# Linear attention by chunk states, and its 32-row products two heads at a time, in a two-block network

## The chip, the cores and the metric

The kernel runs on one core of a Trainium2 chip. The metric is the device time of one launch in microseconds (us): 3082.91 us in the median of three runs (3081.30 to 3084.93). Times inside the launch come from one profiled execution, whose span from the first to the last instruction is 3080.9 us. PE is the matrix engine, DVE the vector engine, ACT the scalar engine, POOL GpSimd, SP the engine that issues most transfers.

## The reference, cut to what matters

The network has two blocks of two layers each over 512 tokens of width 1024. In each layer of the first block a mixing stage computes four branches side by side; the second of them is a gated linear attention with 4 heads (keys of 32, values of 64), run forward and backward over the tokens:

```python
def gla_scan(q, k, v, log_a, include_diag):
    def step(state, inp):
        qc, kc, vc, ac = inp
        b = jnp.cumsum(ac, axis=2)
        o_inter = jnp.einsum('bhtk,bhkv->bhtv', qc * jnp.exp(b), state)
        ...
        scores = jnp.einsum('bhtk,bhsk,bhtsk->bhts', qc, kc, decay)
        o = o_inter + jnp.einsum('bhts,bhsv->bhtv', scores, vc)
        b_last = b[:, :, -1:, :]
        state = jnp.exp(b_last[:, :, 0, :])[..., None] * state + \
            jnp.einsum('bhsk,bhsv->bhkv', kc * jnp.exp(b_last - b), vc)
        return state, o
...
    o_f = gla_scan(q, k, v, la_f, True)
    o_b = flip(gla_scan(flip(q), flip(k), flip(v), flip(la_b), False))
    o = (o_f + o_b).transpose(0, 2, 1, 3)
```

The other branches are a short convolution, a softmax attention of 4 heads and a convolution of width 31 with a layer norm. An output product, two layer norms and a feed-forward follow. The second block (attention over selected keys, a mixture of experts) is not touched.

## The kernel before

Everything in the mixing stage of a layer is traced by four generators that `merge` runs side by side, the one furthest behind its share next: `linear` (share 36), `mla` (the softmax attention, 29), `convolutions` (112, with the projections of the input) and `output` (18). The tile scheduler then sets each engine's order from that trace. A `Lane` holds the tiles of one generator: lane G of the linear attention has two banks of PSUM (`ps=2`), lanes A and M two each.

`gla_scores` makes A[s, head, t], the product of query t with key s under the decays between them, for all pairs of tokens by the largest power-of-two boundary between them. There are nine levels, m = 1, 2, ..., 256. For each, ACT takes exponentials (L937 to L942), DVE multiplies them onto q and k (L939, L943), and POOL and ACT bring the running sums to the next level (L957 to L970). In the seven levels below 128, `diag` makes 16 PE products per level (L906): per head, one bank with four blocks of 128 x 128 out of 32 rows (`tile_position=(32 * h, 0)`), then one DVE copy under a mask (COPY_PREDICATED, L913; at level 1 an ACT copy, L910, and L911). The levels 128 and 256 keep their scaled q and k as `far`.

`gla_out` handles one tile of 128 tokens: for each head three 32-row products against the other three tiles (L989), an ACT copy of them (L991), then one product of the tile's own scores with the values (L996) and three of the copied ones (L999), 64 columns each; then the norm and gate.

Operands here are in f32, and each f32 product of the program is two MATMUL records in the trace. The large products (L364 to L366, `mm3`) are three products of split halves, one record each. In a mixing stage these are the projections (`AP<-g,hi`), the output product (`AP<-hi,g`, 192 of them: `out_part` for two of the branches, then for the other two) and the values.

The width-31 convolution is 62 steps on DVE (L776, L778). Its layer norm starts on PE with L786 and on DVE with L789; the output product of its branch begins after that. `attended` and `output` close the stage.

Of the kernel before, what the change touches and what calls it, by code (L numbers as in the profile page):

```python
# [16 lines left out]
OP = mybir.AluOpType  # L17
# [31 lines left out]

def tok_units(w, c, kp):  # L50
    """Rows of two k tiles and 512 columns of w as a moving unit [128, 2 * 512]."""
# [8 lines left out]
def cols(v):  # L60
    """[n * 128] -> [128, n]"""
# [7 lines left out]
def layout(i):  # L69
# [66 lines left out]
    # second block  # L136
# [58 lines left out]
def shape_constants():  # L195
# [14 lines left out]
    # frequency, phase (of a cosine), sign  # L210
# [10 lines left out]
    c["rconst"] = r  # L221
    c["iota"] = np.broadcast_to(p.astype(np.float32), (128, 128))
# [26 lines left out]
def pipeline(n, *stages):  # L249
    """Stage s of item i beside stage s + 1 of item i - 1."""  # L250
# [8 lines left out]
class Lane:  # L259
    """Tiles of one chain of work: its own slots, so that chains do not wait for each other's."""  # L260
# [27 lines left out]
class Net:  # L288
# [20 lines left out]
    def part(self, name):  # L309
        """Room on chip for a part of the work."""  # L310
# [6 lines left out]
    def phase(self, name):  # L317
        """The same with banks of PSUM."""
# [3 lines left out]
    # ---- small helpers  # L322
# [9 lines left out]
    def room(self, dt):  # L332
        """Small tiles in one of the raw ones, until it is full."""
# [15 lines left out]
    def new_h(self):  # L349
        """Token-major tiles [4][128, 1024]."""  # L350
# [3 lines left out]
    def row(self, L, name, n):  # L354
        """A row of DRAM on every partition."""
# [5 lines left out]
    def mm3(self, ps, a, b, start, stop):  # L361
        """ps (+)= a.T @ b for operands (high, low)."""
# [5 lines left out]
    def split(self, hi, lo, src, engine=None):  # L368
        """hi + lo = src, in parts that the PE carries exactly."""
# [3 lines left out]
    def rsqrt(self, L, v, n, scale=1.0, add=EPS):  # L373
        """(v * scale + add) ** -0.5 of [128, n] (more than 0)."""
# [26 lines left out]
    # ---- layer norm of token-major tiles into token-major h and feature-major (high, low)  # L401
# [10 lines left out]
    def ln_norm(self, L, t, gb, spill=None, light=()):  # L412
        """The layer norm of h[t], in place."""
# [3 lines left out]
    def ln_stats(self, L, src):  # L417
        """Of rows in two halves: what normalises them."""
# [1586 lines left out]
```

## Time and profile before

| what | value |
|---|---|
| median of three runs | 3082.91 us (3081.30 to 3084.93) |
| profiled execution, first to last instruction | 3080.9 us |
| PE busy | 2959.6 us (96%) |
| DVE busy | 2155.6 us (70%) |
| ACT busy | 1432.6 us (46%) |
| POOL busy | 463.6 us (15%) |
| mixing stage of layer 0, first product of `diag` to the feed-forward | 63.52 to 330.21 us |
| the same of layer 1 | 742.75 to 1006.03 us |

The busy time of PE over the span says that it is seldom without work, not that every stage is limited by it. So each mixing stage is read in four stretches, cut where the work changes: from the first `diag` product to the input of the wide convolution (L731); from there to the layer norm behind it (L789); to the first output product; and to the feed-forward. For each the profile gives the busy time of every engine and the granted clock of PE.

### The profile page before, as it was taken

What the parts mean: (1) busy time and instruction counts of PE and PEld (TensorE: products, weight loads), DVE (VectorE), ACT (ScalarE), POOL (GpSimd) and SP (SyncE); (2) the same over time, 40 slices, a digit from 0 to 9 for tenths busy, and PEclk for the clock granted to TensorE, in tenths of its full rate; (3) what the DMA queues carried; (4) which work ended last, traced back from release to release, by engine and by line L of the source; (5) the groups of instructions that cost most, each with busy time, mean ns of one, the idle gap of its engine ahead of it and who ended that gap; (6) DMA issues with size and microseconds to landing.
All of it is one profiled execution on the core that took longest, in us unless ns stands there. A gap on an engine that the chain in (4) does not pass through costs nothing. (4 is left out here: it accounts for less than half of the span.)

```text
span 3080.9 us, 38491 instructions
## 1 busy us (share of the span) xinstructions
PE 2959.6 (96%) x14258; PEld 2306.5 (75%) x14258; DVE 2155.6 (70%) x3441; ACT 1432.6 (46%) x2230; POOL 463.6 (15%) x427
## 2 busy tenths in 40 slices
PE   7999999999999999999999997999899999979996
PEld 6777888888777888887777786777577777867774
DVE  6884756565976755666875447999758754479997
ACT  4443433334344433324534433888445344238884
POOL 4311100004211000011101103110311011031103
PEclk9999999998999999999999998999899999989998
DMA  5121233333120332335232256999441322569993
GB/s 185 50 74 42 84 96 96 99 115 104 49 76 28 104 97 97 101 130 158 59 94 75 82 205 222 366 385 384 163 143 57 93 78 83 198 221 358 384 382 123
DMA packets 128512, 457.25 MB, mean 148 GB/s; under 512 B 15744, under 2 KB 16832, under 8 KB 126912
## 3 DMA queue, kind: packets, MB, share of 16 engines
q1 hardware_dynamic: 117696, 425.37, 40.0%
q0 software_dynamic: 7168, 16.79, 1.7%
q10 hardware_dynamic: 3456, 12.58, 1.1%
q8 instruction: 114, 1.87, 0.2%
q14 instruction: 78, 0.64, 0.1%
HBM read 428.99 MB, written 27.26 MB: 148 GB/s over the span
## 5 line engine op out<-in xcount | busy, mean ns | idle before, releaser
L364 PE MATMUL AP<-g,hi 128*128 128x512 f32 (+1 forms) x1824 | 712.7, 391 | 6.1 <-DVE g L1321 2.6
L365 PE MATMUL AP<-g,hi 128*128 128x512 f32 (+1 forms) x1824 | 703.0, 386 | 3.7 <-DVE g L371 3.7
L366 PE MATMUL AP<-g,lo 128*128 128x512 f32 (+1 forms) x1824 | 703.9, 386 | 0.0
L371 DVE TENSOR_TENSOR lo<-raw,hi 128x1024 fp32r<-128x1024 f32 x306 | 393.5, 1287 | 373.2 <-ACT hi L370 364.1
L370 ACT CAST hi<-raw 128x1024 fp32r<-128x1024 f32 x318 | 333.5, 1050 | 607.0 <-PE AP L365 406.7
L364 PEld LDWEIGHTS AP<-g,hi 128*128 128x128 f32 x1824 | 346.9, 190 | 81.8 <-issue 8.2
L365 PEld LDWEIGHTS AP<-g,hi 128*128 128x128 f32 x1824 | 347.2, 190 | 71.5 <-issue 4.3
L366 PEld LDWEIGHTS AP<-g,lo 128*128 128x128 f32 x1824 | 346.9, 190 | 68.8 <-issue 2.6
L371 DVE TENSOR_TENSOR lo<-g,hi 128x1024 fp32r<-128x1024 f32 x204 | 239.1, 1218 | 23.7 <-ACT hi L370 23.2
L370 ACT CAST hi<-g 128x1024 fp32r<-128x1024 f32 x204 | 207.0, 1050 | 50.5 <-PE AP L366 32.7
L371 DVE TENSOR_TENSOR lo<-wide,hi 128x1024 fp32r<-128x1024 f32 x180 | 211.0, 1217 | 23.9 <-ACT hi L370 23.4
L365 PE MATMUL HP<-lo,Txt 128*96 128x512 f32 x512 | 203.7, 398 | 0.0
L366 PE MATMUL HP<-hi,Txt 128*96 128x512 f32 x512 | 203.5, 397 | 0.0
L364 PE MATMUL HP<-hi,Txt 128*96 128x512 f32 x512 | 201.5, 400 | 1.1 <-ACT Txt L370 1.1
L370 ACT CAST hi<-wide 128x1024 fp32r<-128x1024 f32 x180 | 182.7, 1050 | 22.3 <-PE HP L366 18.3
L364 PE MATMUL AP<-hi,g 128*128 128x512 f32 x384 | 159.6, 419 | 2.7 <-DVE g L880 2.7
L366 PE MATMUL AP<-hi,g 128*128 128x512 f32 x384 | 152.9, 400 | 0.0
L365 PE MATMUL AP<-lo,g 128*128 128x512 f32 x384 | 152.3, 398 | 0.0
L364 PE MATMUL BP<-hi,g 128*128 128x512 f32 x352 | 136.8, 390 | 0.0
L365 PE MATMUL BP<-lo,g 128*128 128x512 f32 x352 | 136.6, 389 | 0.0
L366 PE MATMUL BP<-hi,g 128*128 128x512 f32 x352 | 134.0, 389 | 0.0
L1203 POOL TENSOR_TENSOR Bw<-Bw,Bw 128x512 f32<-128x512 f32 x26 | 43.7, 1681 | 459.0 <-DVE Bw L1202 384.0
(497 smaller groups left out, 5235.3 us busy)
## 6 DMA issues: line engine op xcount, KB each, us to landing
wide<-in_wmoeu SPq DMA_DIRECT2D x64, 1024.0 KB, 8.5
g<-in_wmoeu SPq DMA_DIRECT2D x64, 1024.0 KB, 8.1
raw<-in_wup SPq DMA_DIRECT2D x88, 512.0 KB, 3.5
g<-in_wmoed SPq DMA_DIRECT2D x34, 1024.0 KB, 8.6
wide<-in_wmoed SPq DMA_DIRECT2D x30, 1024.0 KB, 8.2
raw<-in_xwin SPq DMA_DIRECT2D x50, 512.0 KB, 3.7
raw<-in_xgate SPq DMA_DIRECT2D x48, 512.0 KB, 3.6
raw<-in_wdown SPq DMA_DIRECT2D x44, 512.0 KB, 3.5
```

Of the source, the lines that this page charges most:

```text
L364: mm(ps, a[0], b[0], start=start, stop=False)
L365: mm(ps, a[0], b[1], start=False, stop=False)
L366: mm(ps, a[1], b[0], start=False, stop=stop)
L370: self.nc.scalar.copy(hi, src)
L371: (engine or self.nc.vector).tensor_tensor(out=lo, in0=src, in1=hi.bitcast(F32), op=OP.subtract)
L1203: nc.gpsimd.tensor_tensor(out=u, in0=u, in1=sw, op=OP.add)
```

## The change

Two things change, both in the first block's linear attention.

The scores are made within chunks of 128 tokens alone: the loop ends with level 64, and `far` and its products (L989, L991, L999) are gone. In their place stand states. `gla_scores` also makes `inter`: k and q under the decays to the ends and from the beginnings of their chunk, of 384 columns for each direction. The new `gla_states` turns three chunks of k per direction (three transposes, one ACT copy), makes the product of keys and values of each chunk (all four heads in one product of 128 x 256), and carries the sum along: DVE adds the decayed state before, POOL multiplies by a mask `hmask` that keeps each head's own block; the first state of a direction is masked by DVE. `gla_out` then needs one or two products of 128 rows with 256 columns and four products of the tile's own scores. The mask is one more constant that is loaded.

`diag` takes two heads in turn: block t of the first head, block t of the second, each head in a bank of its own, held in that order by `issue_after`.

```diff
-        merge((linear(), 36), ...
+        merge((linear(), 31), ...
...
-            for h in range(4):
-                ps = L.P((128, NT, 128))
-                r = slice(32 * h, 32 * h + 32)
-                for t in range(NT):
-                    nc.tensor.matmul(ps[:, t, :], K[r, ...], Q[r, ...], ..., tile_position=(32 * h, 0))
+            for h0 in (0, 2):
+                heads = [(h, slice(32 * h, 32 * h + 32), L.P((128, NT, 128))) for h in (h0, h0 + 1)]
+                mm = None
+                for t, (h, r, ps) in itertools.product(range(NT), heads):
+                    with self.tc.issue_after(mm.ins) if mm else nullcontext():
+                        mm = nc.tensor.matmul(ps[:, t, :], K[r, ...], Q[r, ...], ..., tile_position=(32 * h, 0))
...
-        while m < S:
+        while m < 128:
...
+        ends = L.s([128, 2, NT])
+        ac.activation(ends[:, 0], chunks(FP)[:, :, 127], AF.Exp, scale=T)
+        ac.activation(ends[:, 1], chunks(BS)[:, :, 0], AF.Exp, scale=T)
+        inter = self.g8()
+        for i, (src, by, c) in enumerate(((FS, k, first), (BP, k, last), (FP, q, last), (BS, q, first))):
+            ac.activation(inter[:, i, c], src[:, c], AF.Exp, scale=T)
+            ve.tensor_tensor(out=inter[:, i, c], in0=inter[:, i, c], in1=by[:, c], op=OP.mult)
...
+    def gla_states(self, L, inter, ends, gv):
+        st = self.g8(shape=(128, 6, 256))
+        for d, order in enumerate(((0, 1, 2), (3, 2, 1))):
+            pt = L.P((128, 3, 128))
+            for i, b in enumerate(order):
+                nc.tensor.transpose(pt[:, i], inter[:, d, b * 128:(b + 1) * 128], self.ident)
+            kt = L.w((128, 3, 128))
+            ac.copy(kt, pt)
+            for i, b in enumerate(order):
+                ps = L.P((128, 256))
+                nc.tensor.matmul(ps, kt[:, i], gv[b], start=True, stop=True)
+                s = st[:, 3 * d + i]
+                if i == 0:
+                    ve.tensor_tensor(out=s, in0=ps, in1=self.hmask, op=OP.mult)
+                else:
+                    ve.scalar_tensor_tensor(s, st[:, 3 * d + i - 1], ends[:, d, b:b + 1], ps, op0=OP.mult, op1=OP.add)
+                    po.tensor_tensor(out=s, in0=s, in1=self.hmask, op=OP.mult)
...
-            for i, s in enumerate(ss_t):
-                nc.tensor.matmul(ps[:, i * 128:(i + 1) * 128], K[r, ...], Q[r, ...], ..., tile_position=(32 * h, 0))
-            ac.copy(at[:, h], ps)
...
+        far = [(2, t - 1)] * (t > 0) + [(3, 5 - t)] * (t < NT - 1)
+        for i, (a, b) in enumerate(far):
+            nc.tensor.matmul(ps, inter[:, a, ts], st[:, b], start=i == 0, stop=False)
...
-            nc.tensor.matmul(out, ATd[:, h, ...], gv[t][...], start=True, stop=False)
-            for i, s in enumerate(ss_t):
-                nc.tensor.matmul(out, at[:, h, i * 128:(i + 1) * 128], gv[s][...], start=False, stop=i == 2)
+            nc.tensor.matmul(ps[:, h * 64:(h + 1) * 64], ATd[:, h, ts], gv[t][...], start=False, stop=h == 3)
```

In the built programs nothing moves on any engine outside of the two mixing stages, but for the one constant load. Inside them, three places matter.

PE, in the last stretch of layer 0's mixing stage before (GP is a bank of lane G, g the scaled q and k or the copied scores, Gv the values, MP and O the softmax attention's banks):

```order
L1072 MATMUL MP_2244<-g_770,g_769 128x512
L1095 MATMUL O_2236<-Mw_2198,Mv_773 64x128
L989 MATMUL GP_2222<-g_1599 128x128 x3
L996 MATMUL GP_2227<-Gv_586,g_593 128x64
L999 MATMUL GP_2227<-Gv_587,g_2166 128x64
L999 MATMUL GP_2227<-Gv_584,g_2166 128x64
L999 MATMUL GP_2227<-Gv_585,g_2166 128x64
L996 MATMUL GP_2227<-Gv_586,g_593 128x64
```

And what a tile of tokens is now, ahead of the first output product (L365 here, `AP` on the last row), with one product of the convolution's statistics between (L558):

```order
L1016 MATMUL GP_1975<-g_1496,g_1452 128x256 x2
L1019 MATMUL GP_1975<-Gv_588,g_595 128x64 x4
L1091 MATMUL MP_2249<-g_772,g_771 128x512
L558 MATMUL AP_1759<-ones,Cw_1755 128x1
L365 MATMUL AP_1829<-hi_1807,g_1610 128x512
```

Of the 96 products L989 and the 128 products L996 and L999 of both layers, the last stretches held 84 and 128; now they hold 2 products with a state and 8 with the tile's own scores, and the rest stands in the stretch ahead of them.

PE, two heads of one level, layer 0, before (Gw are the scaled k and q; each row of four blocks is a head):

```order
L366 MATMUL AP_1045<-hi_935,g_94 128x512
L906 MATMUL GP_1082<-Gw_1074,Gw_1075 128x128 x4
L906 MATMUL GP_1088<-Gw_1074,Gw_1075 128x128 x4
L1056 MATMUL MP_858<-Mw_551,g_221 128x512
L1056 MATMUL MP_864<-Mw_551,g_221 128x512
```

Now, block by block in two banks (L911), the first three of eight in a row behind two products of the projections:

```order
L367 MATMUL AP_1208<-g_92,lo_1205 128x512
L365 MATMUL AP_1208<-g_92,hi_1204 128x512
L911 MATMUL GP_1132<-Gw_1124,Gw_1125 128x128
L911 MATMUL GP_1133<-Gw_1124,Gw_1125 128x128
L911 MATMUL GP_1132<-Gw_1124,Gw_1125 128x128
```

The two heads of a pair now alternate; the number of separate runs of such products on PE is 51 in both layers, where it was 42.

DVE, in the stretch of the wide convolution, before (L778 is a step of it, L913 the masked copy of a head's scores, L714 and L715 the gate of the values):

```order
L714 SCALAR_TENSOR_TENSOR Gv_590<-Gv_590,AP_1045 128x256
L778 SCALAR_TENSOR_TENSOR cacc_1634<-pad_903,vec_213,cacc_1634 128x512
L913 COPY_PREDICATED g_593<-gmask,GP_1082 128x512
L778 SCALAR_TENSOR_TENSOR cacc_1587<-pad_765,vec_213,cacc_1587 128x512
L913 COPY_PREDICATED g_593<-gmask,GP_1088 128x512
L715 TENSOR_TENSOR Gv_590<-Gv_590,Gv_216 128x256
```

Now (L780, L919, L716 and L717 are the same lines):

```order
L717 TENSOR_TENSOR Gv_591<-Gv_591,Gv_218 128x256
L780 SCALAR_TENSOR_TENSOR cacc_1668<-pad_905,vec_215,cacc_1668 128x512
L780 SCALAR_TENSOR_TENSOR cacc_1632<-pad_767,vec_215,cacc_1632 128x512
L780 SCALAR_TENSOR_TENSOR cacc_1668<-pad_905,vec_215,cacc_1668 128x512
L919 COPY_PREDICATED g_595<-gmask,GP_1055 128x512
L919 COPY_PREDICATED g_595<-gmask,GP_1056 128x512
L780 SCALAR_TENSOR_TENSOR cacc_1632<-pad_767,vec_215,cacc_1632 128x512
```

The copies of a pair stand together or one or two instructions apart, with steps of the convolution around them; none was added or taken away.

## Rows read from the trace of the kernel before

**Rows 1.** Windows, layer 0: us; PE, PEld, DVE, ACT, POOL busy; clock, DMA, GB/s
```profile
63.52:88.16 24.64, 20.56 (x93) 16.08 (x93) 19.68 (x23) 15.32 (x30) 16.52 (x19) 0.86 0.17 57
88.16:205.83 117.67, 117.65 (x589) 89.66 (x590) 111.42 (x173) 43.48 (x94) 26.66 (x26) 0.96 0.22 70
205.83:223.53 17.70, 14.26 (x84) 9.21 (x83) 12.38 (x32) 9.39 (x20) 1.56 (x2) 0.89 0.10 41
223.53:330.21 106.68, 103.89 (x602) 82.63 (x603) 60.76 (x134) 44.64 (x95) 18.05 (x22) 0.92 0.11 35
```

**Rows 2.** The same windows of layer 1, second and fourth stretch
```profile
766.00:881.85 115.85, 112.46 (x561) 86.43 (x562) 112.97 (x170) 44.21 (x94) 24.67 (x24) 0.97 0.21 68
...
899.40:1006.03 106.63, 103.84 (x602) 82.62 (x603) 60.77 (x134) 44.63 (x95) 18.05 (x22) 0.92 0.11 35
```

**Rows 3.** DVE groups of 88.16 to 205.83: busy us, mean ns, idle before
```profile
L778 DVE SCALAR_TENSOR_TENSOR cacc<-pad,vec,cacc 128x512 f32<-128x512 f32 x60 | 46.7, 802 | 0.4
L913 DVE COPY_PREDICATED g<-gmask,GP 128x512 f32<-128x512 uint8 x23 | 16.4, 727 | 0.5 <-PE GP L906 0.4
```

**Rows 4.** PE groups of 223.53 to 330.21: records, busy us, mean ns
```profile
L999 PE MATMUL GP<-Gv,g 128*128 128x64 f32 x96 | 16.3, 308 | 0.0
L989 PE MATMUL GP<-g 32*128 32x128 f32 x84 | 11.2, 292 | 0.6 <-ACT g L991 0.6
...
L996 PE MATMUL GP<-Gv,g 128*128 128x64 f32 x32 | 6.9, 300 | 0.0
```

**Rows 5.** PE in order of time, last stretch of layer 0: start us, us
```profile
267.53 1.26 PE L989 MATMUL GP<-g 32*128 32x128 f32 x12
268.72 0.50 PE L364 MATMUL AP<-hi,g 128*128 128x512 f32 x1
...
271.53 0.93 PE L989 MATMUL GP<-g 32*128 32x128 f32 x6
272.39 0.43 PE L996 MATMUL GP<-Gv,g 128*128 128x64 f32 x2
272.67 0.83 PE L999 MATMUL GP<-Gv,g 128*128 128x64 f32 x6
273.33 0.39 PE L996 MATMUL GP<-Gv,g 128*128 128x64 f32 x2
...
285.80 0.64 PE L996 MATMUL GP<-Gv,g 128*128 128x64 f32 x2
286.23 1.49 PE L999 MATMUL GP<-Gv,g 128*128 128x64 f32 x6
287.51 0.63 PE L996 MATMUL GP<-Gv,g 128*128 128x64 f32 x2
```

**Rows 6.** PE: a product of 256 columns and a transpose, with what follows
```profile
125.54 1.02 PE L1037 MATMUL MP<-g,Mw 128*128 128x256 f32 x4
126.21 0.59 PE L366 MATMUL AP<-hi,g 128*128 128x512 f32 x1
126.64 0.40 PE L364 MATMUL AP<-hi,g 128*128 128x512 f32 x1
...
208.28 0.65 PE L1082 MATMUL T<-c_ident,Mw 128*128 128x128 f32 x4
208.77 1.84 PE L557 MATMUL AP<-ones,Cw 128*128 128x1 f32 x16
```

**Rows 7.** PE: products of diag, one head alone and two adjacent
```profile
63.52 1.15 PE L906 MATMUL GP<-Gw,Gw 32*128 32x128 f32 x8
64.61 0.50 PE L365 MATMUL AP<-g,hi 128*128 128x512 f32 x1
...
77.20 2.07 PE L906 MATMUL GP<-Gw,Gw 32*128 32x128 f32 x8 [4.07 <-ACT g L910]
...
132.42 1.71 PE L906 MATMUL GP<-Gw,Gw 32*128 32x128 f32 x16
134.06 1.12 PE L1056 MATMUL MP<-Mw,g 128*128 128x512 f32 x2
```

**Rows 8.** PE in 205.83 to 223.53: where it waits
```profile
217.48 1.12 PE L1072 MATMUL MP<-g,g 96*128 96x512 f32 x2 [1.66 <-ACT Mw L1017]
...
220.74 2.07 PE L1072 MATMUL MP<-g,g 96*128 96x512 f32 x2 [1.36 <-ACT Mw L1017]
```

**Rows 9.** POOL and DVE on tiles of 128 x 256: busy us, mean ns
```profile
L957 POOL TENSOR_TENSOR g<-g 128x256 f32<-128x256 f32 x8 | 7.7, 966 | 0.1
...
L715 DVE TENSOR_TENSOR Gv<-Gv,Gv 128x256 f32<-128x256 f32 x4 | 2.1, 524 | 0.0
```

More of the change, by code (lines that the diff above doesn't have):

```diff
@@ L814, in linear @@
         def linear():
[L815 removed]
+            ATd, inter, ends = yield from self.gla_scores(G, q, k, dec)
             while "values" not in ready:
                 yield None
[L818 removed]
+            st = yield from self.gla_states(G, inter, ends, gv)
             for t in range(NT):
[L820 removed]
+                yield from self.gla_out(G, t, ATd, inter, st, gv, gm)
                 q2, sq = G.v(), G.s([128, 1])
@@ L901, in diag @@
         def diag(Q, K, lv):
-            for h in range(4):
-                ps = L.P((128, NT, 128))
-                r = slice(32 * h, 32 * h + 32)
-                for t in range(NT):
-                    nc.tensor.matmul(ps[:, t, :], K[r, t * 128:(t + 1) * 128], Q[r, t * 128:(t + 1) * 128],
-                                     start=True, stop=True, tile_position=(32 * h, 0))
-                dst = ATd[:, h, :].rearrange("p (t x) -> p t x", t=NT)
-                if lv == 1:
-                    ac.copy(dst, ps)
-                    ve.copy_predicated(dst, mask(0), own[:, :, h:h + 1].to_broadcast([128, NT, 128]))
-                else:
-                    ve.copy_predicated(dst, mask(lv), ps)
+            for h0 in (0, 2):
[3 more added lines that the diff above has]
+                    with self.tc.issue_after(mm.ins) if mm else nullcontext():
+                        mm = nc.tensor.matmul(ps[:, t, :], K[r, t * 128:(t + 1) * 128], Q[r, t * 128:(t + 1) * 128],
+                                              start=True, stop=True, tile_position=(32 * h, 0))
+                for h, _, ps in heads:
+                    dst = ATd[:, h, :].rearrange("p (t x) -> p t x", t=NT)
+                    if lv == 1:
+                        ac.copy(dst, ps)
+                        ve.copy_predicated(dst, mask(0), own[:, :, h:h + 1].to_broadcast([128, NT, 128]))
+                    else:
+                        ve.copy_predicated(dst, mask(lv), ps)
         mask = lambda lv: self.gmask[:, lv:lv + 1, :].to_broadcast([128, NT, 128])
@@ new lines, in gla_scores @@
+            diag(Q, K, lv)
+            n = S // (2 * m)
+            bc = lambda a: a.to_broadcast([128, n, m])
+            nf, nb, ns, np_ = (hw(a, m) for a in (FP2, BS2, FS2, BP2))
+            ftl, ftr = fp[:, :, 0, m - 1:m], fp[:, :, 1, m - 1:m]
+            btl, btr = bs[:, :, 0, 0:1], bs[:, :, 1, 0:1]
+            po.tensor_tensor(out=nf[:, :, 1], in0=fp[:, :, 1], in1=bc(ftl), op=OP.add)
+            ac.copy(nf[:, :, 0], fp[:, :, 0])
+            po.tensor_tensor(out=nb[:, :, 0], in0=bs[:, :, 0], in1=bc(btr), op=OP.add)
@@ new lines, in gla_scores @@
+            ac.copy(nb[:, :, 1], bs[:, :, 1])
+            if m == 1:
+                po.tensor_copy(ns[:, :, 0], ftr)
+                po.memset(ns[:, :, 1], 0.0)
+                po.tensor_copy(np_[:, :, 1], btl)
+                po.memset(np_[:, :, 0], 0.0)
+            else:
+                po.tensor_tensor(out=ns[:, :, 0], in0=fs[:, :, 0], in1=bc(ftr), op=OP.add)
+                ac.copy(ns[:, :, 1], fs[:, :, 1])
+                po.tensor_tensor(out=np_[:, :, 1], in0=bp[:, :, 1], in1=bc(btl), op=OP.add)
+                ac.copy(np_[:, :, 0], bp[:, :, 0])
@@ L973, in gla_scores @@
+            FP, FP2, BS, BS2 = FP2, FP, BS2, BS
+            FS, FS2, BP, BP2 = FS2, FS, BP2, BP
             m *= 2
             lv += 1
-            yield 3.4 if m <= 128 else 1
-        return ATd, far
-    def gla_out(self, L, t, ATd, far, gv, gm):
+            yield 2.4
+        ends = L.s([128, 2, NT])
+        chunks = lambda a: a.rearrange("p (b x) -> p b x", b=NT)
+        ac.activation(ends[:, 0], chunks(FP)[:, :, 127], AF.Exp, scale=T)
+        ac.activation(ends[:, 1], chunks(BS)[:, :, 0], AF.Exp, scale=T)
@@ L981, in gla_out @@
         ss = L.s([128, 4])
[L982 to L1002 removed]
+        ts = slice(t * 128, (t + 1) * 128)
+        ps = L.P((128, 256))
+        far = [(2, t - 1)] * (t > 0) + [(3, 5 - t)] * (t < NT - 1)
+        for i, (a, b) in enumerate(far):
+            nc.tensor.matmul(ps, inter[:, a, ts], st[:, b], start=i == 0, stop=False)
+        yield 0.8
+        for h in range(4):
+            nc.tensor.matmul(ps[:, h * 64:(h + 1) * 64], ATd[:, h, ts], gv[t][:, h * 64:(h + 1) * 64],
+                             start=False, stop=h == 3)
+        yield 0.9
         sq = L.v((128, 4, 64))
```

68 lines of the change are left out of this document (14 added, 54 removed).

## The prediction

> **What bounds the kernel now.** The change touches two stretches of the program, the mixing stages of layers 0 and 1; everything else keeps its order on every engine, so the prediction is a sum over these two. I read the windows first, because the page's share of busy time hides that the stage changes its limit [rows 1, 2]. From the input of the wide convolution to its layer norm DVE is busy 111.42 of 117.67 us in layer 0 and 112.97 of 115.85 in layer 1. PE is busy just as long there, but DVE alone already fills the stretch, and its largest group, the convolution's steps (60 in the window, 46.7 us), waits for nobody [rows 3]. I call this stretch DVE's. In the next, 17.70 us, both have slack (PE 14.26, DVE 12.38): a chain of statistics runs between them. In the last, from the first output product to the feed-forward, PE is busy 103.89 of 106.68 us and DVE only 60.76; layer 1 repeats it to a hundredth. So PE's work in the last stretch is worth its full time, and PE's work in DVE's stretch is worth next to nothing. The first stretch, 24.64 us, has a PE that waits once, 4.07 us, for the ACT copy that frees its bank [rows 1, 7].
>
> **The change part by part, per layer.**
>
> *The far products leave the last stretch.* It holds 84 records of L989, 96 of L999 and 32 of L996 [rows 4]. Their mean durations overlap one another, so I price them by what they keep PE from doing, the distance between starts [rows 5]. L989: twelve records from 267.53 to 268.72 are 1.19 us, 0.10 each; six from 271.53 to 272.39 are 0.86, 0.14 each with the way in. I take 0.12: 84 x 0.12 = 10.1 us. L996 and L999: eight records from 272.39 to 273.33 take 0.94 us, 0.117 each at the full clock; later eight take 1.71 us (285.80 to 287.51), 0.21 each, at half the clock. Four such groups of eight follow one another there, so 96 x 0.117 + 32 x 0.21 = 18.0 us. Together 28 us. Left in the stretch are one product with a state (two records, 0.4 us by the price below) and four with the tile's own scores (eight records, 0.9 us). Net 27 us off PE, in a stretch whose end PE sets. What is late next? DVE: it keeps some 57 us of work (the norm of three of the four token tiles moves ahead) in some 80 us, 70% where it was 57%, and PE waits for its adds more often. PE's own idle time is 2.8 us now; I let it double and grant 2.5 us. Net 24.5 us.
>
> *The clock.* It was 0.92 in that stretch, that is, part of it at 1.2 instead of 2.4 GHz. One of the half-clock passages is the long run of small products around 285 us just priced at 0.21. That run is gone, the output products now lie closer together; beyond what is counted I take 1.5 us, between 0 and 5.
>
> *The states and the remaining products go into the stretch before it.* PE gets six transposes (four take 0.49 us, 0.12 each: 0.7 us), six products of keys and values and five with a state, 22 records of 256 columns. Four such records take 0.67 us and delay the next product by another 0.2 (0.43 from 126.21 to 126.64 against some 0.23), so 0.22 each: 4.8 us [rows 6]. Twelve products with the tile's scores are 24 records at 0.117: 2.8 us. Six products of L989 leave, 12 records, 1.2 us. Sum 7.1 us, against 17.70 - 14.26 = 3.4 us of slack, most of it waits for the softmax [rows 8] that other work can fill. So at least 3.7 us come on top. DVE gets six operations on 128 x 256 at 0.52 us, 3.1 us, and the norms that move here, against 5.3 us of slack. POOL gets four masks of 0.97 us [rows 9]; POOL also takes the roots of the statistics, which queue behind them. I take +4 us. The lower end is 0: some of it fits beside the statistics. The upper end is +10: a state passes PE, DVE and POOL in turn, two carried steps a direction, 2 x (0.44 + 0.52 + 0.97) = 3.9 us and as much again for the other direction, if nothing lay beside it.
>
> *DVE's stretch.* Two levels' multiplications of 512 columns go, four of 384 come, the 24 masked copies stay. That is about 0.5 us less on a full DVE: -0.5.
>
> *Two heads in turn.* One head's eight records take 1.09 us from start to the next product; sixteen of two adjacent heads 1.64 us, where twice the first would be 2.18, so two adjacent heads already run partly at the same time [rows 7]. Alternating can bring sixteen records down to about 8 x 0.11 + 0.25 = 1.1 us. Twelve of a layer's 14 pairs or so lie in DVE's stretch, where this gives PE idle time and no more. Only the pairs before it count: the input of the convolution then comes earlier, and DVE's stretch starts earlier. Two pairs, each 2.2 to 1.1, less the 0.3 us that a run which is cut in two costs: 1.5 us. In layer 0, 16 instead of 20 products stand ahead, and the 4.07 us wait may move; I take 2 us there, between 0 and 6.
>
> *Costed at nothing.* The fewer ACT copies (ACT is busy 44.64 of 106.68 us) and POOL sums are off the path in every stretch. The mask's load is one transfer on SP's queue ahead of the small vectors of the decays, covered by the projections; at most 1 us if they come late.
>
> *Sum.* Layer 0: -24.5 - 1.5 + 4 - 0.5 - 2 = -24.5; layer 1: -24.0 with 1.5 for the pairs. Together -48.5 us. The profiled span of 3080.9 us becomes 3032.4; it lies 2.0 us under the median of the runs, so the time is 3082.9 - 48.5, rounded to 3035 us.
>
> **The rivals.**
>
> *The pairs pay as well.* If PE, not DVE, were the limit of DVE's stretch, halving its diag records there would count: 178 of them at about 0.10 are 18 us, so 8 us a layer after the cost of cut runs, 16 in all: 3019 us. For it: PE is busy 117.65 of 117.67 us there. Against: DVE's queue has an idle time of 0.4 us before its steps in the whole window [rows 3], so PE cannot be what they wait for. The Trainium skill (TensorE: Matmul & The Clock Gate, Part 3, packing small matmuls) holds that products on different row groups run concurrently, and gives 3.07 times for four tiles of 32 rows; this would be its case for a gain. The sixteen records in 1.71 us agree in kind with it, and only DVE's limit stands against the gain.
>
> *The states hold the stretch.* The matrix products of the states wait in PE's order for ACT's copy and for DVE to free a bank, and the conv statistics wait behind them. With +10 us instead of +4 in each layer, and PE waiting 5 us more for DVE in the last stretch, 22 us of the gain go: 3057 us. For it: PE and DVE serve in order, and G has two banks. Against: softmax products lie between the steps.
>
> *Slower: the pairs in lockstep.* A pair holds both banks of lane G, so the next pair waits for both masked copies, 2 x 0.73 us, and the copies for the pair. If DVE had nothing else at each turn, every pair would cost DVE the products' 1.6 us and handing over, some 2 us; 28 pairs are 56 us, more than the gain: 3091 us. It decides from 1.7 us per pair. Against: in DVE's new order at least three steps of 0.8 us stand around nearly every pair of copies.
>
> *The change does nothing of the kind.* Were the two row groups not run side by side, little would change, since the pairs carry 3.5 us. Were the last stretch held by the softmax chain, the gain would stop there: PE waits for it with 2 products about every 3.3 us (217.48 to 220.74) when nothing lies between; the twelve head-tiles left would be 40 us, well below 80. This case comes to at least 3076 us, no measurable change.
>
> **How the numbers follow.** The forecast has 0.64 (its own range 3020 to 3050), the paying pairs 0.10, the states 0.17, no change 0.04, lockstep or another slower case 0.05. The range 3012 to 3060 takes in the forecast with the bounds of its terms, the pairs' case and the states' case, and leaves 0.2 out. About 0.2% (6 us) is what a measurement can tell from no change: faster 0.91, same 0.04, slower 0.05.
>
> **What would show it.** Right: the last stretch some 80 us long with PE still busy over 95%; the stretch before it 20 to 24 us; DVE's stretch within 2 us of 117.7 and 115.9, with PE idle in it for the first time. Wrong: DVE's stretch shorter by 5 us or more (pairs pay); PE waiting in the third stretch for L998 or L1016 by several us (states); DVE idle before L919 by over 1 us a pair (lockstep); a lower granted clock in the last stretch than 0.92.

## The result, and the profile after

The changed kernel takes 3014.64 us (median of 4 runs, 3012.67 to 3018.00) where the kernel before took 3082.11 us beside it: a ratio of 0.9787, interval 0.9775 to 0.9799, or 67.5 us less. The prediction said 3035 us, 48.5 us less. Sign and range hold; the gain is 16 to 19 us larger than the sum. The profiled execution has a span of 3016.2 us, 64.7 us under that of before, with a mean granted clock of 0.981 where it was 0.972; it is that of the slowest of the four runs.

The eight stretches after, layer 0 and then layer 1 (from and to in us, length; busy time of PE, PEld, DVE, ACT, POOL with instructions; granted clock, DMA share, GB/s), to be set against [rows 1, 2]:

```profile
63.52:86.91 23.39, 19.12 (x108) 14.86 (x108) 16.42 (x22) 13.70 (x26) 12.25 (x16) 0.85 0.19 59
86.91:203.78 116.87, 111.76 (x576) 82.30 (x577) 111.54 (x171) 42.58 (x92) 26.32 (x25) 0.97 0.21 69
203.78:223.24 19.46, 19.09 (x118) 14.04 (x116) 16.45 (x41) 10.01 (x21) 6.02 (x8) 1.00 0.26 105
223.24:299.32 76.08, 72.63 (x404) 54.58 (x403) 63.06 (x136) 38.53 (x81) 17.99 (x22) 1.00 0.12 37
710.68:728.14 17.46, 17.16 (x103) 13.57 (x103) 7.19 (x10) 8.05 (x18) 8.12 (x12) 0.90 0.18 61
728.14:842.85 114.71, 110.13 (x573) 81.32 (x574) 110.24 (x171) 42.59 (x94) 26.23 (x27) 0.99 0.24 78
842.85:868.32 25.47, 23.54 (x124) 17.67 (x124) 18.46 (x47) 13.21 (x28) 6.94 (x7) 0.84 0.11 47
868.32:942.24 73.92, 72.75 (x401) 53.91 (x400) 57.61 (x128) 35.86 (x75) 16.22 (x21) 1.00 0.12 36
```

And the two rows of before that [rows 1, 2] leave out, layer 1's first and third stretch:

```profile
742.75:766.00 23.25, 22.99 (x116) 19.08 (x116) 13.28 (x14) 10.48 (x25) 17.41 (x18) 0.77 0.15 45
...
881.85:899.40 17.55, 14.12 (x83) 9.12 (x82) 12.38 (x32) 9.39 (x20) 1.55 (x2) 0.89 0.17 67
```

| stretch | predicted, L0 / L1 | measured, L0 / L1 |
|---|---|---|
| first | -2 / -1.5 | -1.25 / -5.79 |
| DVE's | -0.5 / -0.5 | -0.80 / -1.14 |
| third | +4 / +4 | +1.76 / +7.92 |
| last | -26 / -26 | -30.60 / -32.71 |
| sum | -24.5 / -24.0 | -30.9 / -31.7 |

The rest of the program gives 2.1 us. So the larger part of what the sum lacks lies in the last stretch, and it goes with the clock column: 0.92 before, 1.00 after in both layers. DVE's stretch did what it was to do: it is as long as before, DVE is as full, and PE waits in it. The products of `diag` are cheaper there than before (21.7 us busy for 178 records, with heads one by one, against 16.2 for 176), and that time has become idle time. PE's group in layer 0's second stretch before, then PE's and DVE's groups after (busy us, mean ns, idle before):

```profile
L906 PE MATMUL GP<-Gw,Gw 32*128 32x128 f32 x178 | 21.7, 293 | 0.0
```
```profile
L911 PE MATMUL GP<-Gw,Gw 32*128 32x128 f32 x176 | 16.2, 290 | 0.7 <-DVE Gw L942 0.7
```
```profile
L780 DVE SCALAR_TENSOR_TENSOR cacc<-pad,vec,cacc 128x512 f32<-128x512 f32 x60 | 46.2, 797 | 0.3
L919 DVE COPY_PREDICATED g<-gmask,GP 128x512 f32<-128x512 uint8 x24 | 16.5, 726 | 0.6 <-PE GP L911 0.5
```

And what PE waits for from 60 to 204 us, after (total us, times, longest):

```profile
PE AP L365 <- ACT Mw L707: 4.0, 1, 4.0
PE AP L365 <- DVE Gv L716: 3.0, 1, 3.0
PE MP L570 <- DVE Md L569: 1.1, 2, 1.0
PE GP L911 <- DVE Gw L942: 0.7, 1, 0.7
```

The wait of 4.07 us for the ACT copy of level 1 [rows 7] did not go, it moved: another ACT operation, L707, now ends it. In both kernels ACT has itself waited there for the same operation of DVE (5.02 us for L603 before, 7.16 for L604 after). The steps and the copies of the convolution's stretch stand as in [rows 3], so no pair cost DVE a turn.

### The profile page after: what moved, and what is told of

The parts are those of the page before. It is cut to its first block, busy times and chain, and to the rows that moved or that the text cites. A ratio compares the mean times of both kernels' runs of the same rounds, so it can differ in the third digit from the quotient of the medians.

```text
span 3016.2 us, 37821 instructions
## 1 busy us (share of the span) xinstructions
PE 2893.3 (96%) x13934; PEld 2242.0 (74%) x13934; DVE 2147.2 (71%) x3453; ACT 1415.8 (47%) x2190; POOL 461.4 (15%) x427
## 5 line engine op out<-in xcount | busy, mean ns | idle before, releaser
L365 PE MATMUL AP<-g,hi 128*128 128x512 f32 (+1 forms) x1824 | 710.4, 390 | 13.7 <-ACT Mw L707 4.0
L372 DVE TENSOR_TENSOR lo<-raw,hi 128x1024 fp32r<-128x1024 f32 x306 | 386.8, 1265 | 370.3 <-ACT hi L371 361.6
L365 PEld LDWEIGHTS AP<-g,hi 128*128 128x128 f32 x1824 | 345.7, 190 | 89.9 <-issue 6.0
L372 DVE TENSOR_TENSOR lo<-wide,hi 128x1024 fp32r<-128x1024 f32 x180 | 211.1, 1218 | 23.7 <-ACT hi L371 23.2
L365 PE MATMUL HP<-hi,Txt 128*96 128x512 f32 x512 | 201.2, 400 | 1.1 <-ACT Txt L371 1.1
L365 PE MATMUL AP<-hi,g 128*128 128x512 f32 x384 | 158.9, 417 | 0.3 <-DVE g L882 0.3
L365 PE MATMUL BP<-hi,g 128*128 128x512 f32 x352 | 136.8, 390 | 0.0
```

The lines of the kernel that those rows point to most:

```text
L365: mm(ps, a[0], b[0], start=start, stop=False)
L372: (engine or self.nc.vector).tensor_tensor(out=lo, in0=src, in1=hi.bitcast(F32), op=OP.subtract)
```

## The experiments

Four questions: which of the two parts gives the gain; why the pairs give nothing; what the products across chunks really cost; and what brings PE's clock down.

### Each part alone

`e1_states_alone` is the changed kernel with `diag` as it was, head by head; `e2_pairs_alone` is the kernel before with the pairs.

```diff
-            for h0 in (0, 2):
-                heads = [...]
-                for t, (h, r, ps) in itertools.product(range(NT), heads):
+            for h in range(4):
+                ps = L.P((128, NT, 128))
+                for t in range(NT):
```

> The states as in the changed kernel, but the 32-row products one head after the other as before. Theory (DVE is the limit while the wide convolution runs, so the pairs bring PE idle time there and little else): about 3018 us, 3014 to 3024, against 3014.6 of the changed kernel and 3082 of before; PE without idle time in that stretch. Rival (the pairs pay as well): 3028 to 3036, the pairs being worth 14 to 20 us.

> The kernel before with two heads in turn and nothing else. Theory: 3079 us, 3075 to 3083, with about 5 us of PE idle time a layer in the stretch of the wide convolution and the same last stretch of 106.7 us. Rival (the pairs pay): 3062 to 3068. If the two parts add up, the gains of this run and of the states alone sum to the 67 us of the whole.

Measured: states alone 3020.82 us, ratio 0.9804 (0.9787 to 0.9822); pairs alone 3084.15 us, ratio 1.0006 (0.9995 to 1.0018). The states carry the gain. What the pairs add to them is not to be told from nothing: the two intervals, 0.9787 to 0.9822 and 0.9775 to 0.9799, overlap. The pairs alone came out 1 us above the range of the theory, and far from the rival's. The two gains add up to 58 us, 9 less than the whole; the intervals are too wide to make anything of that. In what follows, the profile of `e1_states_alone` is that of its fastest run (3012.89 us; the other three took 3019.73 to 3022.40).

### Why the pairs give nothing: two engines are full

The prediction said that DVE hides them. To take DVE out of the way, both runs here cut the wide convolution to 12 of its 31 taps, `e5_before_12taps` with the heads one by one, `e6_pairs_12taps` with the pairs.

```diff
-                for j in range(1, 31):
+                for j in range(1, 12):
```

> The kernel before with the wide convolution cut to 12 of its 31 taps: 38 of the 62 steps of DVE per layer are left out (some 30 us of DVE per layer), and the branch is not computed in full. It is the base for the next run. Theory, that DVE alone sets the length of its stretch: DVE's stretch (117.7 and 115.8 us) gets shorter until PE, with 100 to 110 us of work there, holds it: 5 to 15 us less per layer, 3055 to 3073 us in all. Rival, that PE is as full there as DVE (it is busy 117.65 of 117.67 us): the stretch stays within 4 us, 3075 to 3083 us.

> The run before this one with the products of diag two heads at a time in turn, all else as in the kernel before, so with the same 12 taps. Theory, that the pairs do save PE time and DVE hides it in the full kernel: with DVE relieved they pay, 5 to 9 us per layer, 10 to 18 us below the run with 12 taps and heads one by one, and PE's records of diag take some 1.0 to 1.1 us for sixteen. Rival, that the pairs hand back elsewhere what they save (to the granted clock, or to the wait for both banks): within 4 us of it. Second rival, lockstep: 5 us or more above it, with DVE or PE waiting at the pairs.

Measured: with 12 taps 3078.27 us, ratio 0.9991 (0.9981 to 1.0001), no change to speak of, as the rival had it; with 12 taps and pairs 3059.85 us, ratio 0.9931 (0.9913 to 0.9948), 18.4 us less. DVE's stretch, layers 0 and 1, first of `e5_before_12taps`, then of `e6_pairs_12taps`:

```profile
89.13:207.77 118.64, 118.64 (x589) 90.14 (x590) 86.98 (x134) 43.23 (x94) 24.03 (x26) 0.96 0.22 74
...
765.22:876.98 111.76, 111.76 (x573) 85.50 (x573) 87.18 (x133) 43.51 (x95) 25.60 (x27) 1.00 0.22 73
```
```profile
86.98:194.59 107.61, 106.54 (x573) 80.76 (x574) 88.37 (x136) 45.02 (x99) 27.50 (x29) 0.98 0.22 73
...
748.67:857.32 108.65, 106.61 (x573) 79.91 (x574) 89.57 (x135) 45.94 (x102) 30.37 (x31) 1.00 0.23 72
```

With some 25 us less of DVE's work PE is busy for the whole of either stretch: 118.64 us in layer 0, no shorter than before, and 111.76 in layer 1, 4.1 us shorter at a clock of 1.00. With the pairs as well it is 11.0 us shorter in layer 0, where up to 2.6 us of that are the clock (0.96 to 0.98), and 3.1 in layer 1, with the clock at 1.00 already. By the spans the pairs give 15.2 us there (3076.6 against 3061.4), 14.1 of them in these two stretches. So four kernels stand in a square: taps alone -2.4 us, pairs alone nothing, both together -21. Each engine alone holds the stretch, but for the 4.1 us in layer 1; either relief is hidden by the other engine until both come. The forecast (no gain from pairs there, DVE's limit in the way) was right, its sentence that only DVE sets the stretch was half of the truth. That DVE's steps wait for nobody shows that DVE is full, not that PE isn't: the rival's point, PE busy 117.65 of 117.67 us, was true at the same time, and the rival's price, 8 us a layer, is about what the square gives (18.4 / 2 = 9.2 by the medians, 7.6 by the spans).

### What the products across chunks cost

`e8_no_far` is the kernel before without L989, L991 and L999, with nothing in their place. `e9_no_l999` leaves out the products with the values alone, `e10_no_l989` the scores and their copies alone.

Of `e8_no_far`:

```diff
-            for i, s in enumerate(ss_t):
-                nc.tensor.matmul(ps[:, i * 128:(i + 1) * 128], K[r, ...], Q[r, ...], ..., tile_position=(32 * h, 0))
-            ac.copy(at[:, h], ps)
...
-            for i, s in enumerate(ss_t):
-                nc.tensor.matmul(out, at[:, h, i * 128:(i + 1) * 128], gv[s][...], start=False, stop=i == 2)
```

`e9_no_l999` has only the second of these cuts, `e10_no_l989` only the first, and in place of the second

```diff
-                nc.tensor.matmul(out, at[:, h, i * 128:(i + 1) * 128], gv[s][...], start=False, stop=i == 2)
+                nc.tensor.matmul(out, ATd[:, h, s * 128:(s + 1) * 128], gv[s][...], start=False, stop=i == 2)
```

> The kernel before with the products across chunks and what is made of them (L989, L991, L999) left out and nothing in their place, so that only tokens within a chunk see each other in that branch: no states, no pairs. Theory, that the whole gain is these products and the clock they cost in the last stretch: the last stretch 74 to 78 us in both layers at a clock of 0.98 to 1.00, the third 15 to 18 us, in all 3012 to 3022 us, so the states cost 0 to 8 us in the two layers. Rival, that the products give their own 27 us and the better clock comes from the new order of the changed kernel: a last stretch of 80 to 84 us at 0.92 to 0.95, 3024 to 3034 us.

> The kernel before without the products of the scores across chunks with the values (L999; 96 records in each last stretch); their scores (L989, 84 records, 32 rows) and the copies of these (L991) stay, and nothing reads them. Theory, that the 32-row products bring the clock down in the last stretch: with them there it stays at half speed for 15 to 24 us per layer, the stretch loses 11 to 14 us, 3052 to 3062 us in all. Rival, that the 64-column products do: half speed for 0 to 7 us, the stretch loses 18 to 24 us, 3036 to 3046 us. Second rival, that only both in one long run do: as the rival here, and in the next run as well.

> The kernel before without the scores across chunks (L989) and their copies (L991); the 64-column products with the values (L999) stay and take scores of the same chunk that were there before, so that their result is not the branch's. Theory, that the 32-row products bring the clock down: half speed for 0 to 7 us in each last stretch, which loses 18 to 24 us, 3036 to 3046 us in all. Rival, that the 64-column products do: 15 to 24 us at half speed, the stretch loses 10 to 13 us, 3054 to 3064 us.

Measured: without both 3033.76 us, ratio 0.9850 (0.9834 to 0.9867); without L999 3059.90 us, 0.9931 (0.9915 to 0.9948); without L989 and L991 3030.27 us, 0.9842 (0.9823 to 0.9862). Third and last stretch of layer 0, of `e8_no_far`, `e9_no_l999` and `e10_no_l989` in this order:

```profile
205.42:226.54 21.12, 18.35 (x104) 13.50 (x103) 16.06 (x49) 11.25 (x29) 7.85 (x9) 0.81 0.29 119
226.54:302.13 75.59, 72.13 (x390) 53.65 (x390) 58.29 (x120) 35.41 (x71) 13.03 (x16) 0.99 0.12 36
```
```profile
204.84:222.86 18.02, 14.59 (x84) 9.42 (x82) 12.37 (x32) 9.39 (x20) 1.56 (x2) 0.85 0.20 82
222.86:317.01 94.15, 90.62 (x506) 67.24 (x506) 62.72 (x137) 45.04 (x95) 19.32 (x23) 0.97 0.15 46
```
```profile
205.55:231.21 25.66, 25.66 (x193) 22.42 (x191) 16.09 (x46) 11.96 (x28) 5.03 (x7) 0.93 0.23 95
231.21:306.68 75.47, 72.00 (x399) 53.68 (x398) 59.13 (x123) 35.26 (x71) 15.62 (x19) 1.00 0.12 37
```

Three things are to be seen. Without any product across chunks the last stretch is 75.59 us long, with the states it is 76.08: the whole gain of the last stretch is the work that left it and the clock that came back with it, and the new order adds nothing to it. Second, the products with the values alone take 12.5 us with them (106.68 to 94.15). That is close to 96 records at the 0.117 us that the prediction took, 11.2, but it does not confirm the price, since some 5.7 of the 12.5 us are the clock (0.92 to 0.97). Third, a surprise: without the scores and their copies all 96 records of L999 per layer are still made, and the kernel is as fast as without them. They no longer wait for L991, so 92 of the 96 of layer 0 slide into the third stretch, where the statistics leave PE waiting; that stretch is 25.66 instead of 21.12 us, with PE busy throughout, and the last one is as short as with none. So what held these products in the expensive stretch was the scores and copies ahead of them (the two were left out together, so which of them is not shown), and in the cheaper place a good half of their price is hidden. The time is below the ranges of both sides, which had left the products where they were.

The total of `e8_no_far` came out as its rival had it, its last stretches as the theory had them (75.59 and 75.04 us). The difference lies ahead of them: layer 1's second stretch has 120.46 us at a clock of 0.93, and the third ones, with less work than in the changed kernel, 21.12 and 21.02. In the profiled executions the clock's shortfall over the eight stretches (1 minus the clock, times the length, summed) is 29 us there and 10 in `e1_states_alone`, which does more work and is 20.6 us faster by the spans and 13 by the medians.

As to the clock, the theory (32-row products alone bring it down) got the time of `e9_no_l999`, but not its ground: 0.97 of 94.15 us is some 6 us at half the clock (2 x 0.03 x 94.15), not 15 to 24. In the clock, though not in the time, its second rival fits better, that only both kinds of products in one run bring it down.

### What the states cost

`e11_no_states` is the changed kernel without `gla_states` and L1016; the scaled k and q are made, and nothing reads them.

```diff
-            st = yield from self.gla_states(G, inter, ends, gv)
...
-        for i, (a, b) in enumerate(far):
-            nc.tensor.matmul(ps, inter[:, a, ts], st[:, b], start=i == 0, stop=False)
```

> The changed kernel without the transposes, states and products with them (all of gla_states and L1016), so that only tokens within a chunk see each other in that branch; the scaled k and q for them are still made, pairs and the order of the rest stay. Theory, that the states stand mostly in time that PE and DVE waited through before: the third stretch gets 1 to 4 us shorter per layer, 3006 to 3013 us in all. Rival, that they cost what their work adds up to there: 5 to 9 us per layer, 2996 to 3004 us. Second rival, that without them the clock and the waits give it all back, as in the kernel before without its products across chunks (3034 us, where the states alone came to 3021): within 3 us of the changed kernel or slower.

Measured: 3019.15 us, ratio 0.9811 (0.9784 to 0.9837), no faster than the changed kernel, as the second rival had it, though its four runs spread over 15 us (3012.62 to 3027.65). Its third stretches:

```profile
205.04:226.40 21.36, 16.37 (x96) 11.99 (x94) 17.42 (x53) 12.51 (x33) 7.54 (x10) 0.84 0.16 64
...
842.62:862.90 20.28, 17.30 (x116) 12.77 (x116) 15.88 (x52) 10.79 (x29) 8.62 (x10) 0.96 0.40 161
```

PE has 2.7 us less to do in layer 0 than with the states (16.37 against 19.09), and the stretch is 1.9 us longer, at a clock of 0.84 instead of 1.00. Without the states PE waits there (2.6 us in one wait for DVE's L1094, 2.2 in one for ACT's L1034). So the states stand in time that PE waited through. In layer 1 the changed kernel's third stretch is 25.47 us, 5.2 longer than without them, at a clock of 0.84; but in `e1_states_alone`, whose states are the same, both third stretches are 18.76 us at 1.00, with PE busy for all of it:

```profile
207.21:225.97 18.76, 18.76 (x129) 15.61 (x128) 14.85 (x42) 8.79 (x20) 8.07 (x8) 1.00 0.36 146
...
843.45:862.21 18.76, 18.76 (x129) 15.61 (x128) 14.86 (x42) 8.79 (x20) 8.06 (x8) 1.00 0.39 157
```

And `e2_pairs_alone`, which has no states, is as slow in the same place of layer 1:

```profile
872.77:898.16 25.39, 22.99 (x109) 16.79 (x110) 13.44 (x35) 9.39 (x20) 2.58 (x3) 0.65 0.14 54
```

At the full clock the stretch with the states is thus 1.1 to 1.8 us longer than before them, and most of the 7.9 us of layer 1 are not theirs: 4.1 are the clock (0.16 x 25.47) and 1.9 a wait for ACT's L1036.

### What brings the clock down

The first theory after the result was that small products as such do: the last stretch had 212 records across chunks and of own scores, and the clock fell during them. `e3_extra_small` adds 13 products of 64 columns (26 records, nothing reads them) behind the last product of each of the 8 output parts of a layer; `e4_extra_large` adds as many of 512 columns at the same places, one record each; `e7_long_small` puts all 104 small products of a layer in one run (`range(104)` behind one part). The diff is that of the first.

```diff
+        with self.tc.issue_after(last.ins):
+            G, gv = self.spare
+            px = G.P()
+            for j in range(13):
+                self.nc.tensor.matmul(px[:, 0:64], self.ident, gv[t][:, 0:64], start=True, stop=True)
```

> The changed kernel with work put back into the last stretch of each mixing stage: behind each of the eight parts of the output product 13 f32 products of 128 rows and 64 columns whose result nobody reads, 208 records a layer, the number that the far products had there (212). Theory (besides their own time the small products bring the granted clock down): 16 x 26 x 0.117 = 49 us of their own and 10 to 20 us of clock on top, 3073 to 3083 us, with a granted clock of 0.90 to 0.95 in the last stretch instead of 1.00. Rival (the clock passages have another cause, and the far products cost their own time alone): 3060 to 3066 us, clock 1.00.

> The control to the small products: at the same places 13 products of 512 columns of split halves, one record each, unread: 16 x 13 x 0.23 = 48 us, the same time on PE. Theory: 3060 to 3065 us and clock 1.00 in the last stretch, 10 us or more below the kernel with the small ones. Rival (any work there costs the same): within 4 us of the kernel with the small ones.

> The changed kernel with 104 products of 128 x 64 in f32 (208 records, nothing reads them) in one unbroken run per layer, put behind the first products of one output part in the last stretch. The spread ones added earlier, as many, cost 66 us in two layers (3081 us) at a granted clock that stayed near full. Theory, that a long unbroken run of small products is what brings the clock to its lower level in the last stretch of the kernel before: the records of the run reach 0.21 us each within it and the half clock lasts some us beyond: 10 to 25 us per layer at half the clock, 3090 to 3110 us. Rival, that the length of the run has nothing to do with it: 3075 to 3086 us with a last stretch at a mean clock of 0.97 or more.

Measured: spread small products 3081.14 us, ratio 1.0006 (0.9996 to 1.0016); large ones 3083.91 us, 1.0007 (0.9996 to 1.0019); the long run 3067.36 us, 0.9961 (0.9949 to 0.9974). Last stretches of layers 0 and 1, of the three in this order:

```profile
219.72:322.00 102.28, 99.48 (x637) 81.37 (x636) 64.63 (x137) 39.05 (x80) 18.82 (x22) 1.00 0.10 32
...
887.13:994.77 107.64, 103.37 (x635) 84.82 (x636) 63.21 (x135) 36.96 (x77) 19.72 (x23) 0.95 0.10 30
```
```profile
221.11:329.51 108.40, 105.59 (x532) 82.17 (x532) 65.50 (x137) 37.92 (x79) 18.74 (x22) 0.94 0.10 30
...
894.14:1004.19 110.05, 107.24 (x527) 84.08 (x528) 63.94 (x133) 36.80 (x77) 18.59 (x22) 0.91 0.10 27
```
```profile
223.47:322.03 98.56, 95.22 (x613) 77.81 (x612) 63.55 (x137) 38.95 (x81) 18.30 (x22) 1.00 0.10 33
...
890.94:987.20 96.26, 94.72 (x609) 77.54 (x608) 58.34 (x128) 35.39 (x74) 17.41 (x22) 1.00 0.09 28
```

The theory fell. The large ones came within 3 us of the small ones, as the rival had it. The clock stays full with 208 small records more in one run, in both layers, and with the spread ones in layer 0 (0.95 in layer 1, low at the head and at the end of the stretch). It is 0.94 and 0.91 with the large ones, but they do not bring it down. Last stretch of `e4_extra_large`, layers 0 and 1, cut at the first added product, and that product:

```profile
221.11:236.69 15.58, 15.58 (x66) 12.56 (x67) 5.70 (x14) 7.79 (x15) 1.75 (x2) 0.59 0.00 1
236.69:329.51 92.82, 90.01 (x468) 69.61 (x466) 59.80 (x123) 30.14 (x65) 16.99 (x20) 1.00 0.11 35
...
894.14:909.85 15.71, 15.71 (x73) 12.65 (x74) 4.92 (x13) 6.48 (x13) 1.57 (x2) 0.61 0.00 1
909.85:989.40 79.55, 79.22 (x402) 61.68 (x400) 50.30 (x107) 25.07 (x55) 15.74 (x19) 1.00 0.09 27
```
```profile
236.69 3.13 PE L888 MATMUL GP<-hi,g 128*128 128x512 f32 x13
```

The clock is low from the start of the stretch, after PE's waits in the stretch ahead of it (1.36 us in layer 0, 2.48 in layer 1), and full once the added products come; in layer 1 it falls again at the end, from 989.4 us on (0.77), where PE waits three times. So neither the small nor the large products, added there, lower it. The long run came out below the range of either side. The run itself, in order of time (start, us), and its window:

```profile
258.56 0.39 PE L366 MATMUL AP<-lo,g 128*128 128x512 f32 x1
258.78 0.40 PE L367 MATMUL AP<-hi,g 128*128 128x512 f32 x1
259.02 23.33 PE L889 MATMUL GP<-Gv,c_ident 128*128 128x64 f32 x208
282.19 0.39 PE L831 MATMUL GP<-c_ident,Gv 128*128 128x128 f32 x2
```
```profile
259.02:282.19 23.17, 23.17 (x210) 23.17 (x208) 3.99 (x7) 1.19 (x2) 0.00 (x0) 1.00 0.23 70
```

23.17 us without one large product, at a granted clock of 1.00. The kernel before, after its own run of small products [rows 5], looks like this, its last stretch in four pieces, with the last wait ahead of the third:

```profile
223.53:233.30 9.77, 9.77 (x50) 7.50 (x51) 3.47 (x9) 6.47 (x12) 1.19 (x1) 0.68 0.01 3
233.30:284.50 51.20, 50.63 (x327) 40.64 (x327) 24.35 (x52) 17.42 (x40) 5.88 (x7) 1.00 0.19 62
284.50:294.70 10.20, 10.20 (x55) 9.75 (x54) 1.83 (x6) 2.88 (x8) 1.02 (x1) 0.50 0.01 2
294.70:330.21 35.51, 33.28 (x175) 24.73 (x175) 31.11 (x67) 17.87 (x36) 9.96 (x13) 1.00 0.05 16
```
```profile
282.98 0.93 PE L989 MATMUL GP<-g 32*128 32x128 f32 x6 [0.57 <-ACT g L991]
```

From 284.5 us on it is 1.2 GHz for 10 us although PE never pauses, after a piece with L989's 32-row records, L1095's products and a wait of 0.57 us for ACT's copy. This passage costs 5.1 us (0.50 x 10.20). Another 3.1 us are lost at the head of the stretch, as in `e4_extra_large` after waits in the stretch ahead (1.66 and 1.36 us, [rows 8]). The head is much the same without L999, and the 10 us passage is gone; `e9_no_l999` from the end of its head on:

```profile
231.20:316.50 85.30, 82.28 (x467) 60.77 (x466) 58.97 (x128) 39.05 (x84) 17.61 (x22) 1.00 0.16 49
```

So neither kind of product alone did that: the 32-row products without L999 left the clock full, and so did 64-column products in a run longer than that one. Which of the things that stood together there brings the clock down was not settled.

The long run does settle what PE's time is worth in this stretch. It holds PE for 23.2 us and makes the stretch 22.5 and 22.3 us longer; the kernel as a whole loses 48.8 us by the spans (3065.0 against 3016.2), 44.8 of them in the two last stretches. So work put on PE there counts in full, as the prediction said.

### A version that might beat both

`e12_after_slow` gives two or three more of a layer's splits of projections from DVE to POOL, since DVE is one of the two full engines.

```diff
-        st.slow = (2, *range(6, 20, 3))
+        st.slow = (2, *range(6, 20, 2))
```

> The changed kernel with two or three more of the projections' splits (an operation of 128 x 512) per layer given from DVE to POOL. The two runs with 12 taps say that the pairs pay 9 us per layer once DVE has 30 us less there. Theory, that DVE's queue still sets part of the end of its stretch here: 2 to 4 us less per layer, 3007 to 3012 us. Rival, that PE's products then wait for POOL, which takes longer for a split: 3014 to 3022 us.

Measured: 3015.10 us, ratio 0.9792 (0.9776 to 0.9808), the same as the changed kernel; the time is in the rival's range, though PE's wait for POOL is not what one sees. The first stretches are 20.43 and 15.63 us instead of 23.39 and 17.46, DVE's are 119.85 and 115.76 instead of 116.87 and 114.71: DVE is busy there for 113.48 and 111.03 us, no less than before. Over these two stretches together DVE is busy 129.8 and 117.3 us where it was 128.0 and 117.4, and they are as long as before (140.3 and 131.4 us, where they were 140.3 and 132.2). So this edit did not relieve DVE there, and the question what a relieved DVE would give the changed kernel stays open.

## Why the prediction was right, and where its sum was off

**The last stretch: mechanism right, the clock mis-sized.** The far products' price held: `e8_no_far` takes 31.1 us off the stretch. The clock gives 7.8 of that (0.92 to 0.99) and PE's idle time takes 0.7 back, which leaves 24.0 us for the records at the full clock; the prediction's 28 us for the three lines are 25.0 without the half clock in them. Two terms were off. The clock of 0.92 over 106.68 us is 8.5 us against a full clock (0.08 x 106.68). The sum contained 3.0 of it in the 32 records priced at 0.21 instead of 0.117, and 1.5 as the term of its own; 4 us were left out, and they came in both layers. Most of them are the 3.1 us at the head of the stretch; of its passages at half the clock the prediction named only the long run. The head ran at the full clock in the changed kernel, whose third stretch in layer 0 leaves PE only 0.4 us to wait; that the one follows from the other is not shown by itself. And the 2.5 us granted for DVE's adds: PE's idle time in the stretch went from 2.79 us to 3.45 in layer 0 and down to 1.17 in layer 1, so 1.8 and 4.1 us of the grant came back. Together 5.8 and 8.1 us, against 4.6 and 6.7 measured beyond the sum.

**The clock as a whole** is the term that failed, not in this stretch alone. The clock's shortfall times the length, summed over the four stretches of [rows 1], is 18.6 us before (3.4 + 4.7 + 1.9 + 8.5) and 7.0 after (3.5 + 3.5 + 0 + 0); in layer 1 19.3 and 7.0. So up to 24 us came back with the clock, and the sum had 9 (twice 3.0 + 1.5). The difference, 15 us, is about the size of the miss, which is 14.1 us in the two mixing stages and 2.1 in the rest of the program. It is an upper bound, since a slow PE costs nothing where another engine holds the stretch.

**The third stretch: the lower bound of the step was wrong.** "At least 3.7 us come on top" took PE's slack as the room for new work. In layer 0 1.8 us came on top, at the full clock in `e1_states_alone` 1.1; and without the states it is no shorter. The stretch is a chain of waits; most of the work that stands in them is free, and it also keeps PE from pausing. Of layer 1's 7.9 us 4.1 are the clock. Neither layer fell into the 20 to 24 us that the prediction named as a sign of being right (19.46 and 25.47), and that the two come to 9.7 us, near the 8 of the sum, is luck.

**DVE's stretch and the pairs: right**, within 0.7 us, and for the stated reason, DVE's limit, though not for it alone: PE is as full as DVE. The clause that PE would be idle there "for the first time" holds for layer 0 (0.02 to 5.1 us) and not for layer 1, where it had been idle 3.4 us before [rows 2]. That two heads in turn are cheaper is seen in the changed kernel's row, in order of time:

```profile
838.86 1.15 PE L911 MATMUL GP<-Gw,Gw 32*128 32x128 f32 x14
839.94 2.87 PE L788 MATMUL AP<-cacc,ones 128*128 128x512 f32 x4
```

Fourteen records in 1.08 us, 0.077 each, where eight of one head took 1.09, 0.136 each, and sixteen of two adjacent heads 1.64, 0.103 each [rows 7]. Alternating is thus 1.8 times as fast as one head by itself and 1.3 times as fast as the order that it replaced, as the busy times of the whole stretch say too (21.7 and 16.2 us). With 12 taps that was worth 8 to 9 us a layer. The Trainium skill (TensorE: Matmul & The Clock Gate, Part 3, packing small matmuls) has products on different row groups run concurrently. The trace agrees in kind, with these factors for two groups.

**The first stretch** hit layer 0 (-1.25 against -2) and missed layer 1 (-5.79 against -1.5). That is no gain of the pairs: without pairs, `e1_states_alone` has 18.38 us there at a clock of 0.91, against 23.25 at 0.77 before.

**The rivals.** The pairs did not pay, though PE was as full as the rival said. The states did not hold the stretch: they cost 1 to 2 us where the clock is full. Lockstep did not come: DVE's idle time before the copies is 0.6 us in the whole window.

## What to carry to other kernels

When two engines are both full in a stretch, relieving one may give nothing, as here: relieve both in one trial before calling either optimization worthless. What a product costs depends on where its inputs let it stand; look for what holds it in the stretch that PE sets, and for a chain of waits that would take it for little. And read the granted clock of each stretch beside its busy time, in slices, and see where it falls before naming a cause: here 8.5 us came back with it beside some 23 of work taken out, and the large products that seemed to lower it came only after it had risen.

## What the runs showed of the hardware that was not expected

The granted clock of a stretch can differ between two programs that hold the same instructions there. Layer 1's first stretch in `e9_no_l999` and `e10_no_l989`, both with the code of the kernel before in it:

```profile
730.22:751.79 21.57, 21.57 (x104) 17.75 (x105) 10.28 (x13) 10.28 (x25) 14.02 (x16) 0.76 0.17 50
```
```profile
718.04:734.88 16.84, 16.84 (x104) 14.17 (x105) 11.90 (x13) 10.30 (x25) 15.34 (x17) 1.00 0.19 64
```

The same 104 records on PE by line and shape, no pause in either, and 4.7 us between them, at 0.76 and at 1.00. So differences of some us in one stretch of one profile, as those of the first stretches and of layer 1's third, are not to be put down to an edit without the clock column beside them. And a PE that never pauses is no guarantee of the higher level: the stretch at 0.76 is busy for all of its 21.57 us, and the passage from 284.5 to 294.7 us of the kernel before ran at 1.2 GHz with PE busy for every us of it.
